# An interleaving copy bound by DMA: the first load split into an eighth and the rest

## The chip, the cores and the metric

The kernel runs on one core of a Trainium2 chip. The metric is the device time of one execution in microseconds (us). Over three runs the kernel before took 314.24 to 314.29 us, median 314.29.

## The reference

Two float32 arrays x and y of shape 32 x 256 x 1024 are interleaved, element by element, along the last axis:

```
result = np.zeros((batch, seq, dim * 2), dtype=np.float32)
result[..., 0::2] = x
result[..., 1::2] = y
```

There is no arithmetic: 33.55 MB of x and as much of y are read, and 67.11 MB are written.

## The kernel before

Each array is taken as one flat list and cut into n = 8 tiles of 128 partitions x 8192 elements (32 KiB per partition, 4 MiB in all). A tile of x and the same tile of y give 128 x 16384 elements of the output, which are made and stored in two halves (h = 0 and 1) of 32 KiB per partition each. In on-chip memory stand two tiles for x (`xt`), two for y (`yt`) and two for output halves (`ot`).

Three engines carry the work, each with its own list of instructions, and semaphores order them. SyncE loads (lines 46 and 50 to 58): tile after tile, x, then y, on its DMA queue, q1 in the profile. From tile 2 on it waits until VectorE has used the tile that stood in the buffer (`woven` counts the copies). VectorE (lines 60 to 73) makes four copies per tile: for each half, x into the even columns of `ot` (line 70) and y into the odd ones (line 73). Ahead of line 70 it waits for the x tile (`xsem`, line 65, or `hsem`, line 67, for the second half of the first tile) and for the store that had last used this `ot` (line 69); ahead of line 73, for the y tile. ScalarE stores each finished half on its queue, q10 (lines 75 to 82). Each store is one DMA of 128 rows of 32 KiB, but the very first goes as 8 KiB rows and then 24 KiB rows (`parts`, line 40).

A DMA of 128 rows is spread over the core's 16 DMA engines, 8 rows for each. A row is one packet in the profile's count, and each engine ends its share with a 4-byte packet that counts up the semaphore; so each transfer adds 16 to it.

The opening is special. The first x tile is loaded in two halves, each 16 KiB per partition: the first by SyncE (line 46), the second by ScalarE (line 49), behind a small transfer of 16 rows of 512 bytes straight from x to the output (line 48; a store writes the place again later). After the program is written down, lines 100 to 119 take SyncE's and ScalarE's first DMA (lines 46 and 48) out of the body and put each into the program's opening block, ahead of the point (`Drain`) at which the engines gather for the barrier before the body. So these two issue at once, at 0.00 and 0.12 us, and everything else from 2.03 us on.

Of the kernel before, what the change touches and what calls it, by code (L numbers as in the profile page):

```python
# [3 lines left out]


def _interleave(nc, x, y, out):
    P = 128
    W = 8192
    H = W // 2  # L10

    total = 1
    for s in x.shape:
        total *= s
    n = total // (P * W)
    assert n * P * W == total

    def rows(ap, names, k):
        flat = ap.rearrange("b s d -> (b s d)")
        return flat[k * names : (k + 1) * names].rearrange("(p w) -> p w", p=P)  # L20

    fp32 = mybir.dt.float32
    xt = [nc.alloc_sbuf_tensor(f"xt{b}", [P, W], fp32).ap() for b in (0, 1)]
    yt = [nc.alloc_sbuf_tensor(f"yt{b}", [P, W], fp32).ap() for b in (0, 1)]
    ot = [nc.alloc_sbuf_tensor(f"ot{b}", [P, W], fp32).ap() for b in (0, 1)]

    xsem = [nc.alloc_semaphore(f"xsem{b}") for b in (0, 1)]
    hsem = nc.alloc_semaphore("hsem")
    tsem = nc.alloc_semaphore("tsem")
    ysem = [nc.alloc_semaphore(f"ysem{b}") for b in (0, 1)]  # L30
    woven = nc.alloc_semaphore("woven")
    osem = [nc.alloc_semaphore(f"osem{b}") for b in (0, 1)]

    xs = [rows(x, P * W, k) for k in range(n)]
    ys = [rows(y, P * W, k) for k in range(n)]
    os_ = [rows(out, 2 * P * W, k) for k in range(n)]

    Q = W // 4

    def parts(k, h):  # L40
        return [slice(0, W)] if k or h else [slice(0, Q), slice(Q, W)]

    def stored(k, h):
        return 16 * sum(len(parts(j, h)) for j in range(k))

    nc.sync.dma_start(out=xt[0][:, :H], in_=xs[0][:, :H]).then_inc(xsem[0], 16)
    few = (slice(0, P, P // 16), slice(0, 128))
    nc.scalar.dma_start(out=os_[0][few], in_=xs[0][few]).then_inc(tsem, 16)
    nc.scalar.dma_start(out=xt[0][:, H:], in_=xs[0][:, H:]).then_inc(hsem, 16)
    for k in range(n):  # L50
        b = k % 2
        if k >= 2:
            nc.sync.wait_ge(woven, 4 * (k - 2) + 3)
        if k:
            nc.sync.dma_start(out=xt[b], in_=xs[k]).then_inc(xsem[b], 16)
        if k >= 2:
            nc.sync.wait_ge(woven, 4 * (k - 2) + 4)
        nc.sync.dma_start(out=yt[b], in_=ys[k]).then_inc(ysem[b], 16)

    for k in range(n):  # L60
        b = k % 2
        for h in (0, 1):
            c = slice(h * H, (h + 1) * H)
            if h == 0:
                nc.vector.wait_ge(xsem[b], 16 * (k // 2 + 1))
            elif k == 0:
                nc.vector.wait_ge(hsem, 16)
            if k:
                nc.vector.wait_ge(osem[h], stored(k, h))
            nc.vector.tensor_copy(out=ot[h][:, 0::2], in_=xt[b][:, c]).then_inc(woven, 1)  # L70
            if h == 0:
                nc.vector.wait_ge(ysem[b], 16 * (k // 2 + 1))
            nc.vector.tensor_copy(out=ot[h][:, 1::2], in_=yt[b][:, c]).then_inc(woven, 1)  # L73

    nc.scalar.wait_ge(tsem, 16)
    for k in range(n):
        for h in (0, 1):
            nc.scalar.wait_ge(woven, 4 * k + 2 * h + 2)
            for c in parts(k, h):
                nc.scalar.dma_start(  # L80
                    out=os_[k][:, h * W : (h + 1) * W][:, c], in_=ot[h][:, c]
                ).then_inc(osem[h], 16)

    nc.scalar.wait_ge(osem[0], stored(n, 0))
    used = sorted(s.num for s in [*xsem, hsem, tsem, *ysem, woven, osem[0]])
    assert used == list(range(used[0], used[-1] + 1)), used
    nc.scalar.sem_clear(range(used[0], used[-1] + 1))
    nc.sync.nop(nofuse=True).wait_op(osem[1], stored(n, 1), "sem-ge").then_inc(
        osem[1], -stored(n, 1)
    )  # L90


def kernel(tc, x, y, out):
    nc = tc.nc
    tc.close()
    tc.compile()

    _interleave(nc, x, y, out)

    blocks = nc.main_func.blocks  # L100
    for engine in (mybir.EngineType.SP, mybir.EngineType.Activation):
        opening = blocks[0].instructions
        at, moved = next(
            (b, i)
            for b in blocks[1:]
            for i in b.instructions
            if i.engine == engine and i.opcode == "DMACopy"
        )
        assert not (moved.sync_info and moved.sync_info.on_wait)
        body = at.instructions  # L110
        body.remove(moved)
        gate = next(
            n
            for n, i in enumerate(opening)
            if i.engine == engine and i.opcode == "Drain"
        )
        opening.insert(gate, moved)
        at.instructions = body
        blocks[0].instructions = opening


# [1 line left out]
_INS = ['x', 'y']  # L123
_OUTS = [((32, 256, 2048), 'float32')]


# [23 lines left out]
```

## Time and profile before

| what | value |
|---|---|
| median of the runs | 314.29 us |
| profiled execution, whole | 314.17 us |
| its span, first to last instruction | 312.8 us |
| VectorE busy | 72.0 us, 32 copies of about 2.29 us |
| moved by DMA | 134.23 MB in 4928 packets |
| first half of x, issue to landing (line 46) | 8.6 us |
| small transfer (line 48) | 6.0 us |
| second half of x (line 49) | 17.5 us |
| first copy begins | 8.60 us |
| second copy begins (y has landed) | 21.96 us |
| first store issued | 24.34 us |

The span runs from the first instruction to the last; the profiled execution's own time is 1.37 us more. The profile counts an engine as busy only while it computes; the issue of a DMA is not counted, nor is waiting. For the 16 DMA engines it gives a mean busy share (in a short window it can be above 1, since a packet counts where it begins), the bytes moved per second, and for each queue its packets, its megabytes and the time its packets took as a share of 16 engines' time. Packets behind one another in an engine touch: where an engine always has work, its packets' durations add up to the time.

### The profile page before, as it was taken

The numbers are of one execution on the slowest core, as the hardware profiler recorded it, in microseconds if no ns is written. First come the engines' busy times: TensorE is split into PE (matmuls) and PEld (weight loads), VectorE is DVE, ScalarE is ACT, GpSimd is POOL, SyncE is SP. The second block draws the span as 40 slices with busy tenths as digits, with TensorE's granted clock in tenths as the row PEclk, the third lists the DMA queues.
The fourth block names the chain that finished last, engine by engine and source line by source line (L and its number), as shares of the span: only waits on it lengthen the run. The fifth ranks groups of instructions, "written<-read, shape, count | busy, mean of one in ns | idle before, by whom it ended". The sixth has DMA issues, their size and how long they took to land.

```text
span 312.8 us, 116 instructions
## 1 busy us (share of the span) xinstructions
DVE 72.0 (23%) x32; POOL 0.2 (0%) x4
## 2 busy tenths in 40 slices
DVE  0216000501405023050230503205032050415410
POOL 0000000000000000000000000000000000000000
DMA  8999999999999999999999999999999999999998
GB/s 336 436 436 436 436 402 432 440 457 415 448 423 427 444 402 469 402 469 402 469 402 465 406 448 423 427 444 402 469 402 469 402 469 402 465 406 448 423 432 373
DMA packets 4928, 134.23 MB, mean 429 GB/s; under 512 B 560, under 2 KB 576, under 8 KB 576
## 3 DMA queue, kind: packets, MB, share of 16 engines
q10 hardware_dynamic: 2624, 69.22, 51.3%
q1 hardware_dynamic: 2304, 65.01, 48.5%
HBM read 67.12 MB, written 67.12 MB: 429 GB/s over the span
## 4 chain that ended last, share of the span: by engine, by line
DMA 82%; DVE 12%; issue 0%
DMA out_dram<-ot 76%; DVE ot L73 6%; DMA yt<-in_y_dram 6%; DVE ot L70 6%
## 5 line engine op out<-in xcount | busy, mean ns | idle before, releaser
L70 DVE COPY ot<-xt 128x4096 f32<-128x4096 f32 x16 | 36.7, 2295 | 215.0 <-DMA out_dram<-ot 206.4
L73 DVE COPY ot<-yt 128x4096 f32<-128x4096 f32 x16 | 36.6, 2288 | 11.1 <-DMA yt<-in_y_dram 11.1
L134 POOL MEMSET const-bfloat16-1.0<- 128x1 bf16 x1 | 0.1, 101 | 0.0
L134 POOL MEMSET const-uint8-127<- 128x1 uint8 x1 | 0.1, 101 | 0.0
L134 POOL MEMSET const-float32-0.0<- 128x1 f32 x1 | 0.1, 98 | 0.2 <-issue 0.2
L134 POOL MEMSET const-float32-1.0<- 128x1 f32 x1 | 0.1, 98 | 0.0
## 6 DMA issues: line engine op xcount, KB each, us to landing
out_dram<-ot ACTq DMA_DIRECT2D x15, 4096.0 KB, 34.1
yt<-in_y_dram SPq DMA_DIRECT2D x8, 4096.0 KB, 41.5
xt<-in_x_dram SPq DMA_DIRECT2D x7, 4096.0 KB, 24.3
out_dram<-ot ACTq DMA_DIRECT2D x1, 3072.0 KB, 32.7
xt<-in_x_dram SPq DMA_DIRECT2D x1, 2048.0 KB, 8.6
xt<-in_x_dram ACTq DMA_DIRECT2D x1, 2048.0 KB, 17.5
out_dram<-ot ACTq DMA_DIRECT2D x1, 1024.0 KB, 16.2
out_dram<-in_x_dram ACTq DMA_DIRECT2D x1, 8.0 KB, 6.0
```

The source lines that it names most:

```text
L70: nc.vector.tensor_copy(out=ot[h][:, 0::2], in_=xt[b][:, c]).then_inc(woven, 1)
L73: nc.vector.tensor_copy(out=ot[h][:, 1::2], in_=yt[b][:, c]).then_inc(woven, 1)
L134: nc = _bacc.Bacc("TRN2", target_bir_lowering=False, num_devices=1)
```

## The change

The opening transfer of SyncE is cut in two by columns: an eighth of the tile (1024 of 8192 columns, E), as 128 rows of 4 KiB, then the remaining columns of the first half, as 128 rows of 12 KiB. Both count on `xsem[0]`, so the waits of VectorE for the x tiles of buffer 0 count one transfer more. The block that moves DMAs into the opening now moves two for SyncE, in their order, and one for ScalarE as before. All else is as it was; by the program's order, SyncE has 18 instructions of note instead of 17, the two transfers ahead of its first branch.

```
+    E = W // 8
...
-    nc.sync.dma_start(out=xt[0][:, :H], in_=xs[0][:, :H]).then_inc(xsem[0], 16)
+    for c in (slice(0, E), slice(E, H)):
+        nc.sync.dma_start(out=xt[0][:, c], in_=xs[0][:, c]).then_inc(xsem[0], 16)
...
-                nc.vector.wait_ge(xsem[b], 16 * (k // 2 + 1))
+                nc.vector.wait_ge(xsem[b], 16 * (k // 2 + 2 - b))
...
-    for engine in (mybir.EngineType.SP, mybir.EngineType.Activation):
-        opening = blocks[0].instructions
+    for engine, count in ((mybir.EngineType.SP, 2), (mybir.EngineType.Activation, 1)):
+        for _ in range(count):
+            opening = blocks[0].instructions
...
-        opening.insert(gate, moved)
+            opening.insert(gate, moved)
```

## The prediction, made before the result

> **What bounds the kernel now.** I read the page first: which resource is full, and for how much of the span.
>
> ```profile
> span 312.8 us, 116 instructions
> DVE 72.0 (23%) x32; POOL 0.2 (0%) x4
> ...
> DMA packets 4928, 134.23 MB, mean 429 GB/s; under 512 B 560, under 2 KB 576, under 8 KB 576
> ...
> q10 hardware_dynamic: 2624, 69.22, 51.3%
> q1 hardware_dynamic: 2304, 65.01, 48.5%
> ```
>
> VectorE works for 23% of the span, the 16 DMA engines for 99.8% (51.3 + 48.5, SyncE's queue q1 and ScalarE's q10). So the chain of waits, which alternates between copies and stores, only says which transfer ended last; the time is bytes over rate, plus what the DMA engines lose. Where they lose it, the windows view shows (columns: stretch, its length, VectorE, GpSimd, clock, DMA share, GB/s):
>
> ```profile
> 0.00:1.00 1.00, 0.00 (x0) 0.20 (x4) 1.00 0.00 0
> 1.00:2.00 1.00, 0.00 (x0) 0.00 (x0) 1.00 1.11 279
> 2.00:3.20 1.20, 0.00 (x0) 0.00 (x0) 1.00 0.92 382
> 3.20:8.00 4.80, 0.00 (x0) 0.00 (x0) 1.00 1.00 425
> 8.00:26.00 18.00, 6.34 (x3) 0.00 (x0) 1.00 1.00 432
> 26.00:32.00 6.00, 2.66 (x2) 0.00 (x0) 1.00 0.98 386
> 32.00:60.00 28.00, 2.48 (x2) 0.00 (x0) 1.00 1.02 439
> 60.00:290.00 230.00, 55.98 (x25) 0.00 (x0) 1.00 1.00 433
> ```
>
> From 60 to 290 us the rate is 433 GB/s: 134.23 MB at that rate are 310.0 us. The other 2.8 us of the span are lost in two places: nothing moves in the first microsecond and little in the second, and from 26 to 32 us, when the first store joins the loads, the rate dips to 386. The change touches the first place.
>
> How the loss is made up comes from the packet rows of the DMA view. A queue's share, times 16 engines, times the window, over its packets, is the mean duration of one packet. Three windows: the opening (0 to 3.2 us), settled 16 KiB rows (6 to 7.5), settled 8 and 32 KiB rows (33 to 38).
>
> ```profile
> DMA packets 45, 0.74 MB, mean 230 GB/s; under 512 B 0, under 2 KB 0, under 8 KB 0
> ...
> q1 hardware_dynamic: 45, 0.74, 69.5%
> ```
> ```profile
> q10 hardware_dynamic: 27, 0.44, 68.7%
> q1 hardware_dynamic: 16, 0.26, 40.7%
> ```
> ```profile
> q1 hardware_dynamic: 48, 1.57, 72.8%
> q10 hardware_dynamic: 48, 0.39, 18.5%
> ```
>
> - Settled, 16 KiB: (68.7% + 40.7%) x 16 x 1.5 / 43 = 0.611 us. 32 KiB: 72.8% x 16 x 5 / 48 = 1.213 us. 8 KiB: 18.5% x 80 / 48 = 0.308 us. On one line: 0.302 us per 8 KiB and about 0.006 us per packet.
> - Opening, 16 KiB: 69.5% x 16 x 3.2 / 45 = 0.791 us, or 0.180 above the settled row. Over 45 packets that is 8.1 us, **0.51 us per DMA engine**: a wait for the first data.
> - The same arithmetic on q1 from 26 to 32 us (62 packets, 86.3%) gives 1.336 against 1.213 us, 0.48 us per engine.
>
> So the 2.8 us are about 1.0 before the first packet, 0.35 by which the engines start after the first (the starts spread from 1.0 to 2.0 us in 0.2 us windows), 0.51 wait, 0.48 at the first stores, and the rest behind the last packet.
>
> **The change, part by part.** Durations are of the profiled execution, 314.17 us, of which 312.8 are the span and 1.37 lie around it; it stands 0.12 under the median of the runs, 314.29.
>
> 1. *Bytes.* The two transfers carry the same 2 MiB. Nothing is saved there.
>
> 2. *More packets.* 128 rows of 16 KiB become 128 of 4 KiB and 128 of 12 KiB: 8 more packets for each of 16 engines, at 0.006 us each, 0.048 us, and one more semaphore packet of 0.009 us (the trace's 4-byte packets). Engines are full behind it, so it is all on the path: **+0.06**.
>
> 3. *The wait for the first data.* No row shows a 4 KiB first packet. Bounds: if the wait is a latency that does not ask for the size, it stays (0). If the first row must be read before its write can begin, it goes with the row, to a quarter: 0.51 x 3/4 = -0.38. If all of it went, -0.51. On the other side, the short rows could be worse served: another wait of the same 0.51 at the second transfer would be +0.51. What speaks for the middle one: an early engine's first 16 KiB packet takes about twice its settled 0.611 (17 packets begin before 2.0 us and have 1.05 us on average, with 55.8% of 16 engines in 2 us), as if a read of the row came ahead of its write. What speaks against counting it in full: the end of the run is that of the slowest engine, and those that begin last, after 1.6 us, hardly wait in this trace, so that shorter rows give them little. Between the full 0.38 and nothing for the late ones I take half: **-0.19**. That later rows grow (4 to 12 to 32 KiB) is costed at nothing: in the trace 16 KiB rows are followed by 32 KiB ones from 8 us on, and the rate from 8 to 26 us is the settled 432. If that cover failed, it would cost one longer read, up to 0.6.
>
> 4. *The issue that SyncE makes before the barrier.* One more DMA issue of 0.33 to 0.49 us (the timeline's SP rows at 2.03, 2.41 and 2.89), between the first one (0.00 to 0.36) and its arrival at the barrier. ScalarE issues its small transfer at 0.12 and takes 0.59 for it, so the barrier has been waiting for ScalarE beyond 0.7; SyncE may now come last, and y and the second half of x may be issued up to 0.6 us after 2.03. What covers it: the first half keeps q1 busy until about 6.7 us (8 packets of 0.611 from 1.8), and a transfer issued at 2.6 needs, by the first one's rows, 1.0 to 2.0 us to reach the engines, so 4.6 at worst: **0**, with 2 us to spare. Without that cover it would cost up to 0.6.
>
> 5. *The first copy's wait* now counts two transfers. The copy began at 8.6 us and the next copy waited for y until 21.96, so the first copy has 11.06 us of slack: **0**. Behind the first copy stands only that second copy. Later waits on the same semaphore count one transfer more and are met at the same landing.
>
> The sum: 312.8 + 0.06 - 0.19 = 312.67 span, 314.04 with the 1.37 around it; in medians 314.29 - 0.13 = **314.16 us**.
>
> **The rivals.**
>
> - *The wait is a fixed latency.* Then only step 2 is left: 314.29 + 0.06 = 314.35. For it: the engines' data begins to flow at about the same time whenever they start, as the late ones' short waits show. Against it: the doubled first packets.
>
> - *The engines run dry between the two transfers* (slower). A 4 KiB row is 0.157 us by the line above, so an engine has done its eight in 1.26 us, where eight of 16 KiB gave 4.9. If the second transfer's rows reach it more than 1.26 us after the first's, it stands still; that is the point from which this decides. The price: at most the second transfer's own start as the first shows it, 1.02 us from issue to first packet and 0.51 wait, 1.53 in all; with the 1.02 alone 314.29 + 0.06 + 1.02 = 315.37. For it: both queues issue at once, and ScalarE's 0.59 us for its issue at 0.12 says that such issues hold each other up. Against it: the second issue should follow at about 0.4 us, or 1.0 if ScalarE's gets between, so its rows come 0.4 to 1.0 us behind the first's; and in the trace a transfer already queued follows the one before without a gap (shares of 1.00 from 3.2 to 26 us, over the ends of two transfers). The Trainium skill, "DMA: Bandwidth & Descriptors", section "Rules for kernel authors", asks for at least 1 MiB per DMA, and the change's first has 512 KiB; its section "Anatomy of one DMA" gives (for transfers issued by GpSimd) about 2.0 us fixed per DMA. By that rule, uncovered, the sum would be about 316.3 us; the trace's queued transfers, without a gap, speak against it.
>
> - *More goes than the row's share* (faster). If the whole 0.51 goes and the first stores, which then meet engines in another order, lose less of their 0.48, between half and all: 0.51 + 0.24 - 0.06 = 0.69 to 0.93, so 313.6 to 313.36. For it: both look like a wait for first data of a new kind. Against it: the stores and their rows are not changed.
>
> That the change does nothing of what it says is excluded: in the changed program's order both transfers stand ahead of SyncE's first branch, as the one did.
>
> **How the numbers follow.** Forecast 0.40 (313.9 to 314.29, around 314.16), fixed latency 0.15, dry engines 0.25, more than the share 0.20. About 0.2%, 0.63 us, is what a measurement of this kernel can tell from no change. Below 313.66 lies the last case alone: faster 0.20. Above 314.92 lies that of the dry engines: slower 0.25. The rest is 0.55. The range leaves out the lower part of the fast case (0.08) and the upper part of the slow one (0.12): 313.5 to 315.0.
>
> **What would show it.** In the DMA view of the changed kernel's first 3.2 us, the mean packet against the settled line: 4 KiB packets near 0.16 us apart from the first of each engine, and a total wait below 0.51 us per engine if the forecast holds, equal if the latency is fixed. A window with a share well under 1.0 between 2 and 4 us shows engines run dry. The rate from 60 to 290 us must stay at 433, and the loss from 26 to 32 us near 0.48; if that moves by more than 0.2, the end follows it and not the opening. A later issue of y than 2.03 shows the barrier; the forecast is wrong if the windows behind it lose anything.

## The result, and the profile after

The changed kernel is slower: median 315.07 us over 12 runs, against 314.21 us over 12 runs of the kernel before; the ratio on record is 1.0024 (that of the two medians would be 1.0027), with a 95% interval of 1.0015 to 1.0034. What stands out more is the spread: 314.22 to 316.12 us, where the kernel before keeps to 314.14 to 314.31; none of its 138 runs beside the versions tried here is above 314.55. The granted clock was 1.00 in every run, so the long runs are not those of a slower clock. The forecast was 314.16, and its range ended at 315.0.

The profiled execution of the changed kernel took 314.49 us, 0.32 more than that of before; so it shows less than half of the median's loss. The lines of its page that answer to those shown of before:

```profile
span 313.2 us, 117 instructions
...
DVE 72.0 (23%) x32; POOL 0.2 (0%) x4
...
DMA packets 5072, 134.23 MB, mean 429 GB/s; under 512 B 576, under 2 KB 592, under 8 KB 720
...
q10 hardware_dynamic: 2624, 69.22, 51.2%
q1 hardware_dynamic: 2448, 65.01, 48.6%
```

One instruction more, 144 packets more (128 rows and 16 semaphore packets), the same bytes, and the DMA engines as full as before: 99.8%. The windows, with the columns as in the prediction:

```profile
0.00:1.00 1.00, 0.00 (x0) 0.20 (x4) 1.00 0.01 4
1.00:2.00 1.00, 0.00 (x0) 0.00 (x0) 1.00 0.91 180
2.00:3.20 1.20, 0.00 (x0) 0.00 (x0) 1.00 1.13 454
3.20:8.00 4.80, 0.00 (x0) 0.00 (x0) 1.00 1.03 423
8.00:26.00 18.00, 6.30 (x3) 0.00 (x0) 1.00 1.00 430
26.00:32.00 6.00, 2.69 (x2) 0.00 (x0) 1.00 1.03 393
32.00:60.00 28.00, 2.11 (x1) 0.00 (x0) 1.00 1.02 440
60.00:290.00 230.00, 56.36 (x26) 0.00 (x0) 1.00 1.00 433
```

No window is empty that was full before. Rates in such short windows depend on where a packet begins, so I count packets instead. First the opening 3.2 us, then the stretch from 26 to 32 us (DMA view of the changed kernel):

```profile
DMA packets 191, 0.73 MB, mean 228 GB/s; under 512 B 31, under 2 KB 47, under 8 KB 175
...
q1 hardware_dynamic: 160, 0.72, 70.1%
```
```profile
q1 hardware_dynamic: 64, 2.10, 92.8%
q10 hardware_dynamic: 32, 0.26, 10.5%
```

In the opening, q1 has 128 packets of 4 KiB (175 - 47), 16 of 12 KiB and 16 semaphore packets; settled, these would take 128 x 0.158 + 16 x 0.459 + 16 x 0.009 = 27.7 us, and they took 70.1% x 16 x 3.2 = 35.9. The excess, 8.2 us or **0.51 us per engine, is that of the kernel before** in these 3.2 us. From 26 to 32 us, 64 packets of 32 KiB took 92.8% x 96 / 64 = 1.392 us each against 1.213 settled: 0.72 us per engine, where it had been 0.48.

**Where the last engine ends.** The run ends with the last of 16 engines. The same windows at the end of the kernel before, and of a 316.65 us run of the changed kernel (again2, below); one packet of 32 KiB is a share of 0.15 of a 0.5 us window:

```profile
311.00:311.50 0.50, 0.00 (x0) 0.00 (x0) 1.00 1.82 786
311.50:312.00 0.50, 0.00 (x0) 0.00 (x0) 1.00 0.00 0
312.00:312.50 0.50, 0.00 (x0) 0.00 (x0) 1.00 0.02 0
```
```profile
311.50:312.00 0.50, 0.00 (x0) 0.00 (x0) 1.00 0.76 328
312.00:312.50 0.50, 0.00 (x0) 0.00 (x0) 1.00 0.31 131
312.50:313.00 0.50, 0.00 (x0) 0.00 (x0) 1.00 0.16 66
313.00:313.50 0.50, 0.00 (x0) 0.00 (x0) 1.00 0.00 0
313.50:314.00 0.50, 0.00 (x0) 0.00 (x0) 1.00 0.15 66
```

Before, no engine begins a packet of data after 311.5 us (the 0.02 are semaphore packets). In the long run two begin one after 312.0, one after 312.5, and a single one after 313.5: the last engine is still storing when the other fifteen have stopped.

From the packets' own start times and durations in the trace the whole loss can be added up. For each packet I take its duration less the settled one of its size, sum over a stretch, and divide by 16; and I take the end of each engine's last store packet. In us:

| kernel, time of the profiled run | mean start | excess to 8 us | excess 24 to 60 | later | mean end | last end less mean |
|---|---|---|---|---|---|---|
| before, 314.17 | 1.37 | 0.53 | 0.50 | 0.00 | 312.30 | 0.16 |
| changed, 314.49 | 1.18 | 0.69 | 0.77 | 0.00 | 312.67 | 0.10 |
| changed (again), 314.63 | 1.20 | 0.67 | 0.77 | 0.00 | 312.58 | 0.31 |
| changed (again2), 316.65 | 1.20 | 0.69 | 0.74 | 0.19 | 312.85 | 2.09 |
| changed (again3), 314.46 | 1.24 | 0.60 | 0.77 | 0.01 | 312.57 | 0.16 |

The mean end less these terms (and less 0.005 to 0.06 between 8 and 24 us) is 309.89 before, 309.93 to 309.96 in the first, second and fourth trace of the changed kernel and 310.03 in the third, so the columns account for the differences between these to 0.1 us.

### The profile page after: what moved, and what is told of

Read it like the earlier page. It is cut to its first block, busy times and chain, and to the rows that moved or that the text cites. A ratio compares the mean times of both kernels' runs of the same rounds, so it can differ in the third digit from the quotient of the medians.

```text
span 313.2 us, 117 instructions
## 1 busy us (share of the span) xinstructions
DVE 72.0 (23%) x32; POOL 0.2 (0%) x4
## 4 chain that ended last, share of the span: by engine, by line
DMA 82%; DVE 12%; issue 0%
DMA out_dram<-ot 76%; DVE ot L75 6%; DMA yt<-in_y_dram 6%; DVE ot L72 6%
```

## The experiments

Four theories were named as the runs went on. A: short first rows put the 16 engines out of step (at one moment they stand at different places of their lists of packets). B: the loss is at the first stores. C: a second transfer in the opening costs as such. D: engines take up the second queue (q10) at different places of their packet order, and run out of step from there. In each group the runs of the kernel before on the same chip had a median of 314.22 to 314.28 us, and ratios are against these.

### Which part of the split costs

Changed kernel again: no edit.

> The changed kernel once more, for a second trace and its spread. In the first measurement its runs lay between 314.22 and 316.12 us where the kernel before kept to 314.14 to 314.31. Each theory expects the same spread and a median near 315.0; what is wanted is a second look at where the loss stands. Theory A (short rows let the 16 DMA engines start out of step, and they hinder each other afterwards) expects long packets between 3 and 26 us; theory B (the loss is at the first stores, whose meeting with the loads has been shifted) expects them between 25 and 32 us alone; theory C (the second transfer's issue comes late) expects engines standing still between 2 and 4 us.

Measured: 314.97 us (314.39 to 315.71, 10 runs), ratio 1.0023 (1.0014 to 1.0032). The loss and the spread repeat. The excess stands both before 8 us and after 24 us (table), so theory B alone does not cover it; no engine stood still.

Equal 8 KiB rows:

```
-    E = W // 8
+    E = W // 4
```

> The opening half in two transfers of equal rows, 8 KiB and 8 KiB, both ahead of the barrier. Theory A expects less than the changed kernel's loss, near 314.5 us, with a spread under 1 us, since the first rows are twice as long. If a second transfer in the opening costs by itself (theory C), the loss is the same, near 315.0. Theory B gives no size here.

Measured: 314.23 us (314.13 to 316.28, 12 runs), ratio 1.0006 (0.9996 to 1.0016). The median's loss is gone; one run of 12 is 2 us long. Theory C falls, and theory A had expected about 314.5.

12 KiB rows first:

```
-    for c in (slice(0, E), slice(E, H)):
+    for c in (slice(E, H), slice(0, E)):
```

> The same two transfers in the other order, 12 KiB rows first and then 4 KiB rows: as many transfers, packets and issues, without the short rows at the start. Theory A expects the loss to be gone, 314.2 to 314.4 us with a spread like that of the kernel before; theory C (a second transfer as such) expects near 315.0 again.

Measured: 314.38 us (314.22 to 315.46, 11 runs), ratio 1.0003 (0.9994 to 1.0011). The profiled run was the one of 315.46: its last engine ended 1.26 us behind the mean of all, at 313.74, and the last but one at 312.61. So a long run is one late engine here too, but without 4 KiB rows first such runs are rare: 1 of 11 here and 1 of 12 with equal rows. The 0.13 us of the median are within the noise.

The split by partitions:

```
-    for c in (slice(0, E), slice(E, H)):
-        nc.sync.dma_start(out=xt[0][:, c], in_=xs[0][:, c]).then_inc(xsem[0], 16)
+    for r in (slice(0, 64), slice(64, P)):
+        nc.sync.dma_start(out=xt[0][r, :H], in_=xs[0][r, :H]).then_inc(xsem[0], 16)
```

> The opening half in two transfers cut by partitions, 64 rows of 16 KiB each, both ahead of the barrier: a second issue and a second semaphore packet, but rows as before. Theory A expects the time of the kernel before, 314.2 to 314.3 us; theory C (second transfer as such) expects the loss of the changed kernel, near 315.0.

Measured: 319.92 us (319.45 to 321.01, 4 runs), ratio 1.0186 (1.0170 to 1.0201). A miss of every theory, and no test of them, for another thing happens. Its windows and DMA view from 3.2 to 8 us:

```profile
3.20:8.00 4.80, 0.00 (x0) 0.00 (x0) 1.00 1.03 220
```
```profile
q1 hardware_dynamic: 80, 1.05, 101.8%
q10 hardware_dynamic: 32, 0.01, 1.4%
```

The engines are full and move half: 64 rows of 16 KiB take 101.8% x 16 x 4.8 / 64 = 1.22 us each, twice the settled 0.611. The Trainium skill, "SBUF — State Buffer", section "Door 1", says that partitions 0 to 63 reach only 8 of the 16 ports, about 218 GB/s, and partitions 64 to 127 the other 8. The 220 GB/s of this window agree.

### The second queue

One queue: in the changed kernel (a_oneq) and, as its control, in the kernel before (b_oneq).

```
-    nc.scalar.dma_start(out=xt[0][:, H:], in_=xs[0][:, H:]).then_inc(hsem, 16)
+    nc.sync.dma_start(out=xt[0][:, H:], in_=xs[0][:, H:]).then_inc(hsem, 16)
```

> The changed kernel with the second half of the first x tile issued by SyncE, between the opening transfers and y, instead of by ScalarE; ScalarE's queue then holds only the small transfer until the first store. Theory D: the 16 DMA engines, which in the changed kernel's trace take up the second half of x at 13 to 18 different places of their packet order where before all 16 take it up at the same place, run out of step from there, and the last of them sets the end. With one queue all engines have the same order up to the first store, so theory D expects the loss to be gone: 314.1 to 314.4 us, spread under 0.5 us. Theory A (the short rows themselves scatter the engines' starts, whatever follows) expects the changed kernel's 315.0 us and its spread of over 1 us.

> The control: the kernel before with the same move of the second half of x to SyncE's queue. Both theories expect the time of the kernel before, 314.1 to 314.4 us; the comparison with the run above is against this one.

Measured: 314.40 us (314.22 to 314.98, 11 runs), ratio 1.0005 (0.9996 to 1.0014); the control 314.26 us (314.17 to 314.45, 11 runs), ratio 0.9999 (0.9990 to 1.0008). Most of the loss goes with the second queue. Of the medians' difference 0.14 us stay against the control, and as the two intervals overlap, these are not clear of the noise. Theory A had expected 315.0 here, theory D 314.1 to 314.4 with a spread under 0.5 us (it was 0.76). The profiled run, 314.98 us, again has one engine at 313.28 and the next at 312.64.

Without the small transfer:

```
-    nc.scalar.dma_start(out=os_[0][few], in_=xs[0][few]).then_inc(tsem, 16)
...
-    nc.scalar.wait_ge(tsem, 16)
...
-    for engine, count in ((mybir.EngineType.SP, 2), (mybir.EngineType.Activation, 1)):
+    for engine, count in ((mybir.EngineType.SP, 2),):
```

> The changed kernel without the small transfer of 16 rows of 512 bytes from x to the output, and without ScalarE's wait for it (the output does not need it). In the changed kernel it lands at 3.6 us, between the two opening transfers, where before it landed at 6.0. If its place there is what disturbs the engines, the loss shrinks to under 0.3 us; theories A and D expect 314.8 to 315.2 us still. The second issue before the barrier also no longer competes with ScalarE's.

Measured: 314.51 us (314.18 to 315.15, 11 runs), ratio 1.0012 (1.0003 to 1.0021): seven runs up to 314.55, four of 315.00 to 315.15. The median's loss is 0.26 us instead of 0.72, but the interval overlaps that of the changed kernel (1.0014 to 1.0032), so a part of the small transfer in the loss is likely and not shown. The edit also takes ScalarE's issue out of the opening, and it had no control without the transfer.

Both edits at once (a_clean):

```
-    nc.scalar.dma_start(out=os_[0][few], in_=xs[0][few]).then_inc(tsem, 16)
-    nc.scalar.dma_start(out=xt[0][:, H:], in_=xs[0][:, H:]).then_inc(hsem, 16)
+    nc.sync.dma_start(out=xt[0][:, H:], in_=xs[0][:, H:]).then_inc(hsem, 16)
...
-    nc.scalar.wait_ge(tsem, 16)
...
-    for engine, count in ((mybir.EngineType.SP, 2), (mybir.EngineType.Activation, 1)):
+    for engine, count in ((mybir.EngineType.SP, 2),):
```

> The changed kernel with both edits at once: the second half of x on SyncE's queue, and no small transfer (and no wait for it). Until the first store, one queue alone feeds the 16 DMA engines, so that none can take another order of packets. Apart, the edits left 0.15 us (one queue) and 0.26 us (no small transfer) of the 0.72 us loss. Theory D (engines that take up the other queue at different places run out of step) expects 314.2 to 314.35 us and runs within 0.4 us of each other; theory A (the 4 KiB rows scatter the starts by themselves) expects 314.4 to 314.6 with single runs of 315.

Measured: 314.50 us (314.24 to 315.16, 11 runs), ratio 1.0010 (1.0001 to 1.0019), two runs above 315.1. Until the first store there is one queue alone, so that no engine can take another order, and yet 0.28 us and the late engine remain (in the profiled run of 315.16 us one engine ended at 313.47, the next at 312.70). Theory D is not the whole: moving the load takes most of the loss away, but a part stays with the short rows by themselves, as theory A expected (314.4 to 314.6). Removing the small transfer as well gained nothing over a_oneq. This run had no control either.

### How short, and what comes behind

2 KiB rows first:

```
-    E = W // 8
+    E = W // 16
```

> The changed kernel with a sixteenth first: 2 KiB rows, then 14 KiB rows. Measured so far: 16 KiB rows (kernel before) 314.25 us, 12 KiB first 314.38, 8 KiB first 314.23, 4 KiB first 314.97. If the shortness of the first rows is what counts (theory A), 2 KiB costs more than 4 KiB: 315.3 us or above. If it is the place at which the second queue comes in (theory D), there is no such order, and anything from 314.2 to 315.5 can come.

Measured: 314.53 us (314.29 to 316.19, 11 runs), ratio 1.0018 (1.0006 to 1.0030): eight runs up to 314.58, three of 315.48 to 316.19. A miss for theory A in its simple form: shorter is not worse in the median, though the late runs are as late. In its trace the first packets took only 0.18 us on average, and yet the excess to 8 us is 0.68 us per engine, as in the changed kernel: that loss does not sit in the first packet.

Four transfers of 4 KiB rows:

```
-    for c in (slice(0, E), slice(E, H)):
+    for c in [slice(i * E, (i + 1) * E) for i in range(4)]:
...
-                nc.vector.wait_ge(xsem[b], 16 * (k // 2 + 2 - b))
+                nc.vector.wait_ge(xsem[b], 16 * (k // 2 + 4 - 3 * b))
...
-    for engine, count in ((mybir.EngineType.SP, 2), (mybir.EngineType.Activation, 1)):
+    for engine, count in ((mybir.EngineType.SP, 4), (mybir.EngineType.Activation, 1)):
```

> The opening half as four transfers of 4 KiB rows, all ahead of the barrier: the first rows are as short as in the changed kernel, and none behind them is longer until the second half of x. If the shortness of the first rows is the cause (theory A), the loss is that of the changed kernel, 314.8 to 315.1 us with runs above 315.5. If it is the step from 4 to 12 KiB rows, it is gone: 314.2 to 314.5 us (24 more packets per engine than before cost 0.15 us at 0.006 each).

Measured: 315.11 us (314.83 to 315.66, 5 runs), ratio 1.0032 (1.0019 to 1.0044). The step from 4 to 12 KiB is not needed for the loss; with 4 KiB rows throughout it is as large. (The rows still step to 16 KiB at the second half of x, and there are four transfers here; four longer ones were not run.) By the sum of terms the 24 more packets and 3 more semaphore packets cost 0.14 us (mean end less the terms: 310.03 against 309.89), near the 0.15 expected.

### A long run, packet by packet

The changed kernel twice more, no edit.

> The changed kernel once more, one look, in the hope of a run near its median of 315 or above (the two traces so far are of 314.49 and 314.63 us). If the last engine sets the long runs, one or a few of the 16 engines end 0.5 to 1.5 us behind the mean, as one did in the trace of 12 KiB first (1.24 us); if all engines are slowed together, their ends stay within 0.4 us.

> The changed kernel once more, one look, with the same two expectations: in a long run either one or a few of the 16 engines end 0.5 to 1.5 us behind the mean of all, or all end late together, within 0.4 us of each other.

Measured: 316.65 and 314.46 us, one run each. The long run is the one of the table: the mean end of its engines is 0.18 to 0.28 us later than in the three short ones, but its last engine 1.8 to 2.0 us further behind that mean. Followed back from its last packet, as far as packets can be chained by their times, this engine had one packet of 32 KiB 0.75 us too long at 30.2 us, when the first store joined, and then nine too long by 0.06 to 0.17 us, spread from 43.7 to 178 us. In the kernel before, the excess of all engines after 60 us is 0.002 us per engine; here it is 0.19. So engines that are out of step go on losing long after the opening.

The packets' own times show where. After 60 us, only 36 packets in all 20 traces are more than 0.04 us too long. All are loads (q1), and they stand in seven traces: 22 in again2, the others in again3, rev, a_oneq, a_nofew, a_clean and quarters. The five traces in which one engine ends well behind all others (rev, again2, a_oneq, a_clean, quarters) are among them. The 14 outside again2 begin at 76 to 77, 96 to 97, 116 or 135 us: 0.3 to 0.6 us (two of them 1.7 to 1.8) ahead of a copy that had waited for a store to land. So the later losses fall where one store ends, as the first fell where the stores began. The kernel before goes through the same ends of stores without one such packet.

### Where a gain at the start goes

Equal 8 KiB rows and one queue, the candidate:

```
-    E = W // 8
+    E = W // 4
...
-    nc.scalar.dma_start(out=xt[0][:, H:], in_=xs[0][:, H:]).then_inc(hsem, 16)
+    nc.sync.dma_start(out=xt[0][:, H:], in_=xs[0][:, H:]).then_inc(hsem, 16)
```

> A candidate to beat both kernels: equal 8 KiB rows in two opening transfers, and the second half of x on SyncE's queue. In the trace of the two equal transfers the engines begin 0.19 us earlier on average than in the kernel before and give it back at the first stores (0.69 us per engine there against 0.50). If the give-back comes from engines out of step (theory D), the gain stays: 314.0 to 314.15 us. If the first stores take back whatever the start gains, 314.2 to 314.3.

Measured: 314.27 us (314.17 to 314.48, 11 runs), ratio 1.0002 (0.9993 to 1.0010). No gain: with 8 KiB rows the sum of start and excess to 8 us is 1.69 us (halves) and 1.76 (halves_oneq) against 1.90 before, and the excess from 24 to 60 us is 0.69 and 0.65 against 0.50.

An undivided first store, in the kernel before, with equal 8 KiB rows, and in the changed kernel:

```
-        return [slice(0, W)] if k or h else [slice(0, Q), slice(Q, W)]
+        return [slice(0, W)]
```

> The kernel before with an undivided first store, 32 KiB rows like all others. The engines lost 0.50 us each from 24 to 60 us. If the loss belongs to the divided store's two row lengths, most of it goes: about 313.9 us. If it belongs to the first meeting of loads and stores whatever the rows, the time stays at 314.2 to 314.5.

> Equal 8 KiB rows in two opening transfers, with an undivided first store. Divided, the engines gained 0.21 us per engine by 8 us and gave 0.19 back from 24 to 60 us. If the give-back belongs to the divided store, this runs 0.2 us below the control with the same store; if the first meeting of loads and stores takes it back whatever its rows, the two are equal within 0.05.

> The changed kernel with an undivided first store. If engines out of step lose at the change of the store's row length (the trace of the longest run has its long packets at 30 and 41 to 43 us, where the 8 and the 24 KiB rows begin), the loss against the control with the same store shrinks to under 0.3 us. If they lose at every later change of transfer as well, it stays at 0.6 to 0.8 us, with runs more than 1 us long.

Measured: 314.44 us (314.26 to 315.06, 11 runs), 314.46 us (314.30 to 314.65, 11 runs) and 315.07 us (314.97 to 316.31, 7 runs); ratios 1.0007 (0.9998 to 1.0016), 1.0007 (0.9998 to 1.0016) and 1.0032 (1.0021 to 1.0043). The excess from 24 to 60 us is 0.81, 0.91 and 1.07 us per engine: the divided store saves 0.2 to 0.3 us of it, but the give-back does not belong to it (the first two times are equal), nor does the loss of the changed kernel (0.63 us against its control). One run of b_whole is 315.06 us, so a single long run can come with an undivided opening too.

The first store with 4 KiB and 28 KiB rows, in the kernel before and with equal 8 KiB opening rows:

```
-    Q = W // 4
+    Q = W // 8
```

> The kernel before with the first store as 4 KiB rows and then 28 KiB rows (before: 8 and 24). Undivided, that store's phase cost 0.81 us per engine, with 8 KiB first 0.50. If the cost goes with the length of the first rows, it falls to about 0.35 and the time to 314.1 us. If short rows disturb the engines as they do at the opening of the load, the time rises to 314.4 to 315 us and its runs spread over more than 0.6 us.

> Equal 8 KiB rows in two opening transfers, and the first store as 4 KiB and 28 KiB rows. If the first stores no longer take back the gain of 0.2 us at the start, this beats both kernels, at 313.9 to 314.1 us; if they do whatever their rows, it equals the run above within 0.05 us.

Measured: 314.33 us (314.13 to 314.55, 11 runs) and 314.29 us (314.14 to 314.52, 11 runs); ratios 1.0002 (0.9993 to 1.0011) and 1.0003 (0.9994 to 1.0012). Neither the fall nor the rise came; no version beats the kernel before. The excess from 24 to 60 us was 0.85 and 0.75.

## Why the prediction was wrong, point by point

- **What bounds the kernel: right.** 433 GB/s from 60 to 290 us in both; the end follows what the engines lose.
- **Step 1 (bytes) and step 2 (more packets): right.** Forecast +0.06; the mean end less the other terms rose from 309.89 to 309.93 to 309.96, about +0.05.
- **Step 3 (the wait) failed.** It counted -0.19 us for a wait that shrinks with the first row. The wait stayed, 0.51 us per engine in the opening 3.2 us as before, and to 8 us the excess grew, 0.60 to 0.69 against 0.53. The engines did begin 0.13 to 0.19 us earlier, but start and excess to 8 us together are 1.84 to 1.89 us in the four traces against 1.90 before (and 1.80 to 1.95 in the four traces with one opening transfer, b_oneq, b_whole and b_q8 among them): the term was -0.01 to -0.06, within the scatter of the traces. So the rival of a fixed latency was nearer on this term. The doubled first packet, on which step 3 rested, does not go with the row: before, it was 0.44 us too long (1.05 against 0.611), of which a quarter would be 0.11, but the first 4 KiB packet of each engine took 0.49 us on average in the first trace against a settled 0.158, and 0.43 to 0.64 in the other three. So what it waits for stays open.
- **The sum failed because of what it left out, and this is the step that made the forecast wrong.** It took the engines behind the opening to lose what they had lost before, a change of nothing. The traces show two terms instead: +0.24 to +0.28 us per engine when the first stores join, and the distance of the last engine from the mean, 0.10 to 2.09 us against 0.16. The prediction named the first as what would overturn it ("the loss from 26 to 32 us near 0.48; if that moves by more than 0.2, the end follows it"); the second it used only to halve a gain, not as a cost. The median was not itself traced; from the mean terms, about +0.3, its +0.86 needs a last engine some 0.5 to 0.6 us further behind than before, an estimate that lies between the distances of the four traces.
- **That growing rows cost nothing: not refuted.** Four transfers of 4 KiB rows, with no step to 12 KiB, lose as much (they step to 16 KiB later).
- **Step 4 (the issue before the barrier): right.** y is issued at 2.07 us instead of 2.03; nothing waits for it.
- **Step 5 (the first copy): right.** It began at 9.22 us instead of 8.60, and the next still waited for y, until 21.99 instead of 21.96.
- **The rivals.** The dry engines came out on the side of the result, but not by their mechanism: the DMA share from 2.0 to 3.2 us is 1.13, and the two transfers touch. The fast case had the first stores lose less; they lost more. The Trainium skill, "DMA: Bandwidth & Descriptors", section "Rules for kernel authors", asks for at least 1 MiB per DMA. Two transfers of 1 MiB (halves) indeed lose nothing in the median and 0.5 MiB first does, but 0.25 MiB first (e2k) loses no more than 0.5 (0.28 us in the median against 0.72), so a loss that grows as the first transfer shrinks does not fit. No trace shows the 2.0 us of fixed cost that the prediction took from the Trainium skill: the queued transfers touch, and the split cost about 0.05 us.

What is shown: the loss comes with 4 KiB rows first (0.86 and 0.72 us in the changed kernel, 0.83 in quarters, 0.63 in a_whole; 0.28 with 2 KiB rows), and with 8 KiB rows first it is gone from the median in four kernels. Moving the second half of x off the second queue takes most of it away. It is paid at the first stores and, in the long runs, by single late engines: in five of the six traces of 314.98 us or more (rev, again2, a_clean, a_oneq, quarters; not a_whole, and byrows aside) one engine ends 0.3 to 1.5 us behind the next and sets the end. What is not separated: the length of the first rows and the size of the first transfer change together in all these runs, and the share of the small transfer (0.26 us without it, 0.28 without it and with one queue) is within the noise. What stays open: why an engine that is out of step loses again at the ends of later stores, why 2 KiB first is no worse than 4, and why the first stores take back what the start gains.

## What to carry to other kernels

Where DMA is full for the whole span, add up a trace in four terms: when the engines start, what their packets lose at the start and at each joining of loads and stores, and how far the last engine ends behind the mean; a change that gains on the first term may lose on the last. Here rows of 4 KiB at the head of an opening load cost 0.6 to 0.9 us although the engines started sooner, less where no other queue came in behind them; equal 8 KiB rows did no harm to the median and no good. Try such a split with many runs before keeping it. Look at the spread of the runs beside the median: it was the first sign here that one engine of 16 decides.

## What the runs showed of the hardware that I had not expected

- A split by partitions (64 + 64) halves the rate while it lasts: 220 GB/s with engines full, 5.7 us for 2 MiB; the split by columns costs 0.05 us per transfer of 128 rows.
- One late engine of 16 can end 2.1 us behind the mean of all, in a trace whose share from 60 to 290 us is 1.00 and whose rate there is 433 GB/s, as in the kernel before.
- The first joining of stores and loads costs 0.41 to 1.07 us per engine in 19 of the 20 traces, and 0.05 us in the one whose engines had been slowed in the opening (byrows).
